# The 128 copies of a relative-position table are written from memory to memory, not from an 8-partition tile

## The chip, the core and the metric

One core of a Trainium2 chip runs the whole program as one launch. Its five engines (TensorE for matrix products, VectorE, ScalarE, GpSimd, and SyncE, which issues DMAs) each work through an instruction list of their own in order and wait for each other by semaphores. Data moves between memory and the on-chip SBUF by 16 DMA engines that all issuers share. The metric is the device time of one execution in microseconds (us).

## The reference

The program is one forward pass of two stacked transformer-like blocks on 256 tokens of width 1024, in float32. The stage that matters here is the first block's mixer, which projects the normalised input and feeds four branches:

```
proj = h @ w_in
(m_z, m_xbc, m_dt, b_qkv, c_qkv, c_f, d_q, d_kv, gate_logits) = split(proj)
y_a = mamba2_branch(m_z, m_xbc, m_dt, ...)          # a state-space scan with decays
y_b = moba_attention(bq, bk, bv, rel_bias[:, :8])   # one causal block of 256
y_c = forgetting_attention(cq, ck, cv, c_f + forget_bias)
y_d = sliding_window_attention(dq, dk, dv, sinks, rel_bias[:, 8:])
out = sum(sigmoid(gate_i) * (y_i @ w_branch_i)) @ w_out
```

`y_b` and `y_d` add to each attention score a bias that depends on the head and on the distance of query and key: `bias[h, q, k] = rel_bias[rel_bucket(q - k), h]`, for 8 heads each. For every query the 256 biases are a window of one table of 383 entries per head, shifted by one entry from query to query.

## The kernel before

All weights are streamed from memory in pieces of about 1 MB: SyncE loads a piece into one of four `raw` buffers (L138), ScalarE rounds it to a high part `whi` (L97), VectorE subtracts to get a low part `wlo` (L98), and TensorE makes three products of each pair (L143 to L145). `whi` and `wlo` have four buffers of half a piece each. A `raw` buffer is free for its next load once both halves are split. The order of the instructions on each engine is set by the framework's scheduler when the program is built; on the chip each engine keeps to it.

In the mixer, `mamba` first makes eight 128-column blocks of `m_xbc` (`gemm_b`). For each, VectorE writes the block into `xin` behind three zeros that GpSimd sets (L581, L582), applies a four-tap filter into `cv` (L568, L570), and ScalarE applies silu into `bcT` (four blocks) or `xsT` (four blocks) (L585). Behind these stands the call `then()`, which is `skew_bias`. Then come the products of `bcT` (L591, evicted as `cbm` at L594), the projection `m_z`, and, head by head, the decay factors `mt` from `rows` (L615 to L618). `rows` are the cumulated decays of four heads, which `rows4` has GpSimd load from a small memory array `acd`, once for heads 0 to 3 and once for 4 to 7 (L422). The query, key and value projections of the next branch (`qk`, L456) are interleaved with this.

`skew_bias` makes the bias. For each of the two groups of 8 heads, a product of the one-hot distance table and `rel_bias` gives [8 heads, 383] in PSUM (L382). VectorE copies it to the SBUF tile `rv` on 8 partitions (L384), and one DMA issued by GpSimd writes it 128 times per head into the memory array `skew[g]` (L385), 1024 rows of 1532 bytes. `rv` has one buffer, so the copy of the second group waits until the DMA of the first has read the tile. Later GpSimd loads each attention's bias from `skew` with a row step of 382 entries, which gives each query its shifted window (`bias4`, L432). GpSimd's DMAs are queued on q0; SyncE's on q1.

Of the kernel before, what the change touches and what calls it, by code (L numbers as in the profile page):

```python
# [9 lines left out]
F32 = mybir.dt.float32  # L10
# [6 lines left out]
P = 128  # L17
# [10 lines left out]
def bucket_onehot():  # L28
    """Per distance 255 - v the bucket of a relative position, for whole-block and windowed masks."""
    m = np.zeros((33, 2, NV), np.float32)  # L30
    for v in range(NV):
        d = 255 - v
        b = sum(1 for s in BUCKET_START if s <= max(d, 0)) - 1
        for g, lim in enumerate((256, 128)):
            if 0 <= d < lim:
                m[b, g, v] = 1.0
            else:
                m[32, g, v] = 1.0
    return m
# [8 lines left out]
def pack(inputs):  # L48
    """The program's inputs: the large arrays as they are, the small ones laid out in the columns of one array."""
    data = {n: np.ascontiguousarray(inputs[n]) for n in _INS}  # L50
    cols = []
    for name, n in COLS:
        c = np.zeros((P, n), np.float32)
        if name == "heads":
            c[0:8, 0] = inputs["dt_bias"][0]
            c[32:40, 0] = inputs["forget_bias"][0]
            c[0:8, 1] = inputs["a_log"][0]
        elif name == "rel_bias":
            c[0:32] = inputs["rel_bias"]
            c[32] = NEG  # L60
        elif n == 8 and inputs[name].size == 8:
            c[:] = np.asarray(inputs[name]).reshape(1, 8)
        else:
            c[:] = np.asarray(inputs[name]).reshape(n, P).T
        cols.append(c)
    data["params"] = np.ascontiguousarray(np.concatenate(cols, axis=1))
    w = np.zeros((P, 8, 40), np.float32)
    w[:, :, 0:8] = np.asarray(inputs["w_in"])[0, :, 1536:1544].reshape(8, P, 8).transpose(1, 0, 2)
    w[:, :, 32:40] = np.asarray(inputs["w_in"])[0, :, 4616:4624].reshape(8, P, 8).transpose(1, 0, 2)
    data["w_heads"] = w  # L70
    data["onehot"] = bucket_onehot()
    return data


class Build:
# [28 lines left out]
    def weights(self, dmas, nk, ncols):  # L104
        """Loads [128, nk, ncols] of weights by dmas(raw) and splits them; gives per K tile the pair (hi, lo)."""
        nc = self.nc
        raw = self.wraw.tile([P, 2048], F32, tag="raw", name=self.nm("raw"))
        r3 = raw[:, :nk * ncols].rearrange("p (k c) -> p k c", c=ncols)
        dmas(r3)
        out = []  # L110
        step = max(1, min(nk, 1024 // ncols))
        for k0 in range(0, nk, step):
            n = min(step, nk - k0)
            hi = self.wspl.tile([P, 1024], F32R, tag="whi", name=self.nm("whi"))
            lo = self.wspl.tile([P, 1024], F32R, tag="wlo", name=self.nm("wlo"))
            h3, l3 = (u[:, :n * ncols].rearrange("p (k c) -> p k c", c=ncols) for u in (hi, lo))
            with self.tc.high_priority(offset=400):
                self.split(h3, l3, r3[:, k0:k0 + n], self.split_engine())
            out += [(h3[:, k], l3[:, k]) for k in range(n)]
        return out  # L120

    def split_engine(self):
        """GpSimd takes a share of the weights' low parts where the vector engine has much else to do."""
        self.turn += 1
        if self.burst:
            self.burst -= 1
            return self.nc.gpsimd
        return self.nc.gpsimd if self.share and self.turn % self.share == 0 else self.nc.vector
# [18 lines left out]
    def gemm_a(self, hk, w, chunks, apart=0):  # L147
        """[tok, cols] = h @ w for the column chunks; chunks share the K order, so that early K tiles come first.
        Of the last `apart` K tiles the first token tile takes all before the second does."""
# [24 lines left out]
    def gemm_b(self, hk, w, c0, nblk):  # L174
        """[128 columns, 256 tok] blocks of (h @ w)^T."""
        wk = self.wunit(w, 0, 8, c0, nblk * P)
        return [self.block_b(hk, wk, slice(b * P, (b + 1) * P)) for b in range(nblk)]
# [10 lines left out]
    def norm_input(self, x, n, t, wcol, hi, lo, ss):  # L188
        """x[:, t, n-th half] -> sums of squares and the weighted, split transpose."""
# [17 lines left out]
    def held(self):  # L207
        """The first products of a phase take turns with the last transposes of its input."""
        ins = self.hold.pop(0) if self.hold else None
        return self.tc.issue_after(ins) if ins else nullcontext()  # L210
# [10 lines left out]
    def rstd(self, ss, scale=1.0 / D):  # L221
        """[128, 2] of rsqrt(mean of squares + eps) from the partial sums ss [128, 2, 2]."""
        nc = self.nc
        r = self.small.tile([P, 2], F32, tag="rstd", name=self.nm("rstd"))
        nc.vector.tensor_tensor(r, ss[:, :, 0], ss[:, :, 1], op=ALU.add)
        self.rsqrt(r, r, scale)
        return r
# [9 lines left out]
    def row(self, r):  # L237
        """Returns a function that gives [128, 256]: r of each token along the free axis, on every partition."""
# [19 lines left out]
    def to_T(self, src, hi, lo, t, nblk=4, scale=None, c0=0):  # L258
        """src [128 tok, nblk * 128] -> split transposes hi/lo[:, c0 + j, tokens of tile t]."""
# [15 lines left out]
    def constants(self):  # L275
# [9 lines left out]
        # causal factors for transposed scores: [s0 x l0 | s0 x l1 | s1 x l1]  # L285
# [19 lines left out]
    def swiglu(self, hk, r, wg, g0, wu, u0, wd, x, finish, apart=0):  # L305
        """x += (silu(h wg) * (h wu)) wd, with the norm's factor r applied to the products."""
# [39 lines left out]
    def project(self, hk, w, x, finish):  # L346
        """x += h @ w; the transposes of the first half's sum take place between the second half's products."""
# [12 lines left out]
    def mixer(self, hk, r, rr, x, finish):  # L360
        nc, a, tc = self.nc, self.a, self.tc
        w_in = a["w_in"][0]
        with tc.tile_pool(name="yT", bufs=3) as ytp, tc.tile_pool(name="att", bufs=1) as at, \
# [9 lines left out]
            skew = dr.tile([2, 8, P, NV], F32, name="skew")  # L373

            def skew_bias():
                # relative-position bias, [q, 255 + q - k] laid out along the diagonals
                oh = at.tile([33, 2, NV], F32, tag="pt", name="oh", bufs=1)
                nc.gpsimd.dma_start(oh, a["onehot"])
                rb = self.col["rel_bias"][0:33]
                for g in range(2):  # L380
                    ps = self.tp()
                    nc.tensor.matmul(ps[:8, :NV], rb[:, g * 8:(g + 1) * 8], oh[:, g], start=True, stop=True)  # L382
                    rv = at.tile([8, NV], F32, tag="y", name=self.nm("rv"), bufs=1)
                    nc.vector.tensor_copy(rv, ps[:8, :NV])  # L384
                    nc.gpsimd.dma_start(skew[g], rv.unsqueeze(1).to_broadcast([8, P, NV]))  # L385
# [3 lines left out]
            # m_dt and c_f side by side: [0:8] and [32:40] of one block of columns  # L389
# [85 lines left out]
            # sliding-window queries: block j holds heads j and j + 4  # L475
# [29 lines left out]
            def gate_evict(ps, c0, n, skip=0):  # L505
                """columns c0.. of the gate logits from ps[:, skip:]"""
# [46 lines left out]
    def softplus(self, out, v, e, w, d):  # L553
        """out = max(v, 0) + log1p(exp(-|v|)); the logarithm is corrected for the rounding of 1 + exp."""
# [10 lines left out]
    def conv4(self, out, xin, wcol, bcol):  # L565
        """Causal 4-tap filter along the free axis; xin has three zeros in front."""
# [70 lines left out]
    def attention(self, at, qT, kT, v, bias, own0, sinks, split_heads, yT):  # L637
        """Causal softmax attention of 8 heads of 64; bias(gi) holds bias and mask of a group of four heads."""
# [75 lines left out]
    def hgrn(self, hk, r, rr, x, finish):  # L714
        """Gated linear recurrence as decayed causal attention: pairs (t, s) are split by the level at which
        the halves that hold them part, so that both decay factors to the boundary are at most one."""
# [74 lines left out]
    def hgrn_scores(self, hp, q, k, f, masks, LV):  # L791
        """Transposed decayed scores of four heads.  At level L a token's q carries the decay from the start of
        its block of L tokens, its k the decay to the block's end; pairs in neighbouring blocks meet there."""
        nc = self.nc
        st = hp.tile([P, 4, 2, P], F32, tag="st", name=self.nm("st"), bufs=2)
        # s = t, on every partition; the identity keeps one
# [16 lines left out]
        for L in LV[::-1]:  # L813
# [4 lines left out]
            if L == 1:  # L818
                # neighbours, on every partition
# [55 lines left out]
    def lru(self, hk, r, rr, x, finish):  # L875
        nc, a, tc = self.nc, self.a, self.tc
        w = a["lru_w_in_2"][0]
        with tc.tile_pool(name="lru", bufs=1) as lp:
            cw, cb = self.col["lru_conv_w_2"], self.col["lru_conv_b_2"]
            ba, bx = self.col["lru_ba_2"], self.col["lru_bx_2"]  # L880
            # 8 softplus(-lambda)
# [41 lines left out]
            def decay(g):  # L923
                # a = exp(-c r);  1 - a^2 = tanh(c r) (1 + a^2)
# [43 lines left out]
            # the functions of one table stay together  # L968
# [22 lines left out]
    def body(self):  # L991
        nc, a, tc = self.nc, self.a, self.tc
        with ExitStack() as es:
# [37 lines left out]
            # the first block's final norm is the second block's input  # L1031
# [18 lines left out]
            # with m the mean square of x and m2 that of x * wf: rf^2 = 1 / (m + eps), r^2 = rf^2 / (m2 rf^2 + eps)  # L1050
# [76 lines left out]
```

## Time and profile before

| | |
|---|---|
| time, median of 3 runs | 1235.18 us (1235.17 to 1236.95) |
| span of the profiled execution | 1232.9 us |
| TensorE busy in the span | 1156.8 us (94%) |
| VectorE, ScalarE, GpSimd busy | 753.0, 600.4, 123.8 us |
| moved by DMA | 202.76 MB, mean 164 GB/s |

The span runs from the first to the last instruction of one profiled execution. That execution's own time outside the profiler is not recorded; the median of the timed runs is 2.3 us above the span. TensorE is the busiest engine by far, so what counts is where it stands idle or runs at a lower granted clock. Of the 40 equal slices of the span (30.8 us each), TensorE's busy digits are 8665 in the first four and 9 nearly everywhere else.

### The profile page before, as it was taken

How to read it: one execution, taken by the hardware profiler on the slowest of the kernel's cores; microseconds unless marked ns; L12 is line 12 of the kernel's file. 1: busy time of each engine (PE TensorE's matmuls, PEld its weight loads, DVE VectorE, ACT ScalarE, POOL GpSimd, SP SyncE). 2: the span in 40 equal slices, each digit the busy share in tenths (PEclk: the TensorE clock that was granted, in tenths of full speed). 3: DMA queues.
4: the chain of work that ended last, by engine and by line, in shares of the span. 5: the costliest groups of instructions: out<-in, count | busy, mean ns of one | idle time of the engine just before them, and what ended most of it. 6: DMA issues, size and time to landing. Idle time of an engine off the chain costs nothing.

```text
span 1232.9 us, 15797 instructions
## 1 busy us (share of the span) xinstructions
PE 1156.8 (94%) x6308; PEld 987.8 (80%) x6308; DVE 753.0 (61%) x968; ACT 600.4 (49%) x876; POOL 123.8 (10%) x118
## 2 busy tenths in 40 slices
PE   8665999999999999999999999999998769999997
PEld 7555989888888888888878878888888758888886
DVE  7373656556567555555899665555548795555553
ACT  6142656674445544445552455444445555544442
POOL 1000001000000000003820030000003432000000
PEclk9877999999999999999999999999999889999999
DMA  8676444535555555456443425555553544555550
GB/s 287 125 143 170 144 133 156 190 136 171 189 187 189 178 192 176 156 186 205 137 155 119 137 102 192 185 172 185 175 185 103 171 135 161 196 174 172 187 188 34
DMA packets 120729, 202.76 MB, mean 164 GB/s; under 512 B 4220, under 2 KB 44413, under 8 KB 120656
## 3 DMA queue, kind: packets, MB, share of 16 engines
q1 hardware_dynamic: 117264, 192.59, 47.1%
q0 software_dynamic: 2960, 8.53, 3.8%
q8 instruction: 49, 0.80, 0.3%
q10 hardware_dynamic: 432, 0.63, 0.2%
q14 instruction: 24, 0.20, 0.0%
HBM read 197.51 MB, written 4.23 MB: 164 GB/s over the span
## 4 chain that ended last, share of the span: by engine, by line
PE 82%; DVE 9%; DMA 6%; ACT 2%; issue 1%; SPq 0%; POOLq 0%; POOL 0%; DVEq 0%; ACTq 0%
PE acc L144 25%; PE acc L145 25%; PE acc L143 25%; DMA skew<-rv 3%; DMA raw<-in_w_in_dram 3%; DVE wlo L98 2%; PE tp L263 2%; PE tp L831 2%; DVE uc L570 1%; PE tp L661 1%; DVE hs L941 1%; ACT whi L97 1%; PE tp L690 1%; PE tp L197 1%; DVE sq L930 1%
## 5 line engine op out<-in xcount | busy, mean ns | idle before, releaser
L98 DVE TENSOR_TENSOR wlo<-raw,whi 128x1024 fp32r<-128x1024 f32 (+3 forms) x350 | 423.9, 1216 | 315.1 <-ACT whi L97 310.9
L97 ACT CAST whi<-raw 128x1024 fp32r<-128x1024 f32 (+3 forms) x372 | 382.1, 1032 | 409.9 <-PE acc L145 324.5
L145 PE MATMUL acc<-whi,hl 128*128 128x512 f32 (+2 forms) x832 | 318.2, 383 | 0.0
L144 PE MATMUL acc<-wlo,hh 128*128 128x512 f32 (+2 forms) x832 | 317.4, 382 | 0.6 <-DVE wlo L98 0.6
L143 PE MATMUL acc<-whi,hh 128*128 128x512 f32 (+2 forms) x832 | 313.0, 381 | 0.0
L144 PEld LDWEIGHTS acc<-wlo,hh 128*128 128x128 f32 x832 | 156.8, 188 | 33.2 <-DVE wlo L98 1.6
L143 PEld LDWEIGHTS acc<-whi,hh 128*128 128x128 f32 x832 | 156.9, 189 | 30.7 <-issue 0.3
L145 PEld LDWEIGHTS acc<-whi,hl 128*128 128x128 f32 x832 | 156.9, 189 | 30.2
L143 PE MATMUL acc<-hh,whi 128*128 128x256 f32 (+1 forms) x496 | 142.1, 289 | 27.7 <-ACT xsT L585 20.6
L145 PE MATMUL acc<-hh,wlo 128*128 128x256 f32 (+1 forms) x496 | 142.4, 289 | 3.5 <-DVE wlo L98 3.4
L144 PE MATMUL acc<-hl,whi 128*128 128x256 f32 (+1 forms) x496 | 142.6, 288 | 0.6 <-DVE hl L98 0.6
L143 PEld LDWEIGHTS acc<-hh,whi 128*128 128x128 f32 (+1 forms) x496 | 94.9, 192 | 30.0 <-ACT xsT L585 21.0
L144 PE MATMUL acc<-wlo,ah 128*128 128x512 f32 x264 | 102.5, 391 | 0.0
L145 PE MATMUL acc<-whi,al 128*128 128x512 f32 x264 | 102.0, 390 | 0.0
L143 PE MATMUL acc<-whi,ah 128*128 128x512 f32 x264 | 101.6, 390 | 0.0
L145 PEld LDWEIGHTS acc<-hh,wlo 128*128 128x128 f32 (+1 forms) x496 | 95.1, 192 | 5.2 <-DVE wlo L98 4.7
L98 POOL TENSOR_TENSOR wlo<-raw,whi 128x1024 fp32r<-128x1024 f32 x22 | 56.9, 2595 | 420.9 <-ACT whi L97 420.9
L144 PEld LDWEIGHTS acc<-hl,whi 128*128 128x128 f32 (+1 forms) x496 | 95.6, 193 | 2.6 <-DVE hl L98 1.1
L143 PEld LDWEIGHTS acc<-whi,ah 128*128 128x128 f32 x264 | 49.6, 188 | 10.2
L145 PEld LDWEIGHTS acc<-whi,al 128*128 128x128 f32 x264 | 49.6, 188 | 10.2
L144 PEld LDWEIGHTS acc<-wlo,ah 128*128 128x128 f32 x264 | 49.6, 188 | 10.0
L97 ACT CAST ah<-tp 128x512 fp32r<-128x512 f32 (+1 forms) x36 | 19.8, 550 | 34.6 <-PE tp L263 34.6
(307 smaller groups left out, 1286.1 us busy)
## 6 DMA issues: line engine op xcount, KB each, us to landing
raw<-in_ffn_w_in_dram SPq DMA_DIRECT2D x44, 1024.0 KB, 5.1
raw<-in_w_in_dram SPq DMA_DIRECT2D x33, 1024.0 KB, 5.0
raw<-in_ffn_w_out_dram SPq DMA_DIRECT2D x20, 1024.0 KB, 5.1
raw<-in_hgrn_w_in_dram SPq DMA_DIRECT2D x16, 1024.0 KB, 5.4
raw<-in_w_ffn_gate_dram SPq DMA_DIRECT2D x11, 1024.0 KB, 5.0
raw<-in_w_ffn_up_dram SPq DMA_DIRECT2D x11, 1024.0 KB, 5.0
raw<-in_w_ffn_down_dram SPq DMA_DIRECT2D x10, 1024.0 KB, 4.9
raw<-in_w_branch_dram SPq DMA_DIRECT2D x8, 1024.0 KB, 5.0
```

Source lines behind the costliest of these rows:

```text
L97: self.nc.scalar.copy(hi, src)
L98: (eng or self.nc.vector).tensor_tensor(lo, src, hi.bitcast(F32), op=ALU.subtract)
L143: mm(ps, sh, mh, start=start, stop=False)
L144: mm(ps, sh, ml, start=False, stop=False)
L145: mm(ps, sl, mh, start=False, stop=stop)
L197: last = nc.tensor.transpose(ps[:, j * P:(j + 1) * P], xc[:, j * P:(j + 1) * P], self.ident)
L263: nc.tensor.transpose(ps[:, j * P:(j + 1) * P], src[:, j * P:(j + 1) * P], self.ident)
L570: nc.vector.scalar_tensor_tensor(out, xin[:, k:k + S], wcol[k], out, op0=ALU.mult, op1=ALU.add)
L661: nc.tensor.matmul(ps[par][:, jj * W:(jj + 1) * W], qT[pr, 2 * gi + jj, qt * P:(qt + 1) * P], kT(2 * gi + jj)[pr, :W], start=True, stop=True)
L690: nc.tensor.transpose(ps[:, i * P:(i + 1) * P], sp[:, i, b * P:(b + 1) * P], self.ident)
L831: nc.tensor.matmul(ps[:, c:c + 64], k[:, h, ts], q[:, h, ts].rearrange("p (n u l) -> p n u l", u=2, l=L)[:, :, 1], start=True, stop=True)
L930: nc.vector.tensor_tensor(sq, av[g], av[g], op=ALU.mult)
```

## The change

The two tables are first collected in one tile `rv` of [8, 2, 383], which one DMA writes to a new small memory array `relv`. Two further DMAs then write the 128 copies of each group into `skew[g]`, with `relv` as their source instead of the SBUF tile. The destination, its layout and the loads from it are the same.

```diff
             skew = dr.tile([2, 8, P, NV], F32, name="skew")
+            relv = dr.tile([8, 2, NV], F32, name="relv")
...
                 rb = self.col["rel_bias"][0:33]
+                rv = at.tile([8, 2, NV], F32, tag="y", name="rv", bufs=1)
                 for g in range(2):
                     ps = self.tp()
                     nc.tensor.matmul(ps[:8, :NV], rb[:, g * 8:(g + 1) * 8], oh[:, g], start=True, stop=True)
-                    rv = at.tile([8, NV], F32, tag="y", name=self.nm("rv"), bufs=1)
-                    nc.vector.tensor_copy(rv, ps[:8, :NV])
-                    nc.gpsimd.dma_start(skew[g], rv.unsqueeze(1).to_broadcast([8, P, NV]))
+                    nc.vector.tensor_copy(rv[:, g], ps[:8, :NV])
+                nc.gpsimd.dma_start(relv, rv)
+
+                for g in range(2):
+                    nc.gpsimd.dma_start(skew[g], relv[:, g].unsqueeze(1).to_broadcast([8, P, NV]))
```

The other lines of the diff drop comments. Lines of the changed kernel stand four below those of before from here on (L581 is L585, L432 is L436). The scheduler orders the engines' instructions anew, of which three places follow. The numbers in the tile names below are counters of the build; a tile of the changed kernel has the number of its counterpart or one more.

GpSimd, from the first write of `skew` to the second load of `rows`, with the semaphores that each instruction waits for (`DMASW` is that of a DMA of GpSimd's own), before:

```order
L385 DMA skew<-rv_567 1024x1x383 [waits DVE_49]
L422 DMA rows_676<-acd 128x1024 [waits DMASW1_49]
L581 MEMSET xin_467 128x3 [waits DVE_49,Pool_49]
L581 MEMSET xin_476 128x3 [waits DVE_49,Pool_49]
L432 DMA bias_1109<-skew 128x4x256 [waits DMASW2_49]
L385 DMA skew<-rv_572 1024x1x383 [waits DVE_49]
L581 MEMSET xin_545 128x3 [waits DVE_49,Pool_49]
L581 MEMSET xin_554 128x3 [waits DVE_49,Pool_49]
L422 DMA rows_710<-acd 128x1024 [waits DMASW3_49,DVE_49]
```

and of the changed kernel:

```order
L426 DMA rows_677<-acd 128x1024 [waits DMASW1_49]
L386 DMA relv<-rv 8x766 [waits DVE_49]
L585 MEMSET xin_468 128x3 [waits DVE_49,Pool_49]
L585 MEMSET xin_477 128x3 [waits DVE_49,Pool_49]
L389 DMA skew<-relv 1024x1x383 [waits DMASW3_49]
L389 DMA skew<-relv 1024x1x383
L585 MEMSET xin_546 128x3 [waits DVE_49,Pool_49]
L436 DMA bias_1110<-skew 128x4x256 [waits DMASW4_49]
L585 MEMSET xin_555 128x3 [waits DVE_49,Pool_49]
L426 DMA rows_711<-acd 128x1024 [waits DMASW2_49,DVE_49]
```

The first `rows` load now stands ahead of the writes of `skew`; both of these stand together, behind a wait for `relv`; and one `xin` memset, `xin_555`, now stands behind the first bias load, which waits for the first write of `skew`.

VectorE around the copy of the second table, before:

```order
L98 TENSOR_TENSOR wlo_640<-raw_637,whi_639 128x1024
L582 TENSOR_TENSOR xin_476<-acc_442,rrow_223 128x256
L568 TENSOR_SCALAR cv_470<-xin_467,pcol 128x256
L98 TENSOR_TENSOR wlo_644<-raw_637,whi_643 128x1024
L568 TENSOR_SCALAR cv_479<-xin_476,pcol 128x256
L570 SCALAR_TENSOR_TENSOR cv_470<-xin_467,pcol,cv_470 128x256
L384 COPY rv_572<-tp_570 8x383
L570 SCALAR_TENSOR_TENSOR cv_479<-xin_476,pcol,cv_479 128x256
```

The changed kernel has both copies of `rv` earlier, one behind the other but for one split. The place at which it uses `xin_555` for the first time (`cv_558`) stands between the two halves of the piece `raw_785`, the first of the `qk` weights:

```order
L586 TENSOR_TENSOR xin_546<-acc_496,rrow_224 128x256
L574 SCALAR_TENSOR_TENSOR cv_480<-xin_477,pcol,cv_480 128x256
L572 TENSOR_SCALAR cv_549<-xin_546,pcol 128x256
L586 TENSOR_TENSOR xin_555<-acc_521,rrow_224 128x256
L98 TENSOR_TENSOR wlo_788<-raw_785,whi_787 128x1024
L574 SCALAR_TENSOR_TENSOR cv_549<-xin_546,pcol,cv_549 128x256
L572 TENSOR_SCALAR cv_558<-xin_555,pcol 128x256
L98 TENSOR_TENSOR wlo_792<-raw_785,whi_791 128x1024
L574 SCALAR_TENSOR_TENSOR cv_549<-xin_546,pcol,cv_549 128x256
```

So the filter that needs the memset is ahead of the second half's split `wlo_792` on VectorE.

ScalarE around the last silu of `bcT` (`bcT` of `cv_401` before, of `cv_402` now), before:

```order
L97 CAST whi_639<-raw_637 128x1024
L585 ACTIVATE bcT<-cv_392 128x256
L585 ACTIVATE bcT<-cv_401 128x256
L97 CAST whi_643<-raw_637 128x1024
L97 CAST whi_786<-raw_784 128x1024
```

and of the changed kernel:

```order
L97 CAST whi_640<-raw_638 128x1024
L589 ACTIVATE bcT<-cv_393 128x256
L97 CAST whi_644<-raw_638 128x1024
L621 ACT_TABLE_LOAD
L621 ACTIVATE mt_679<-mt_679 128x384
L621 ACTIVATE mt_687<-mt_687 128x384
L589 ACT_TABLE_LOAD
L589 ACTIVATE bcT<-cv_402 128x256
```

The exponentials of `mt` for the first two heads, with a table load ahead and another behind, now stand in front of the last `bcT`. On TensorE the products of `bcT` stand at the same place among the `m_z` products in both.

## Rows read from the trace of the kernel before

**Rows 1.** The first line of the page of the kernel before, and its part 4: the chain that ended last, by engine and by line, as shares of the span.

```profile
span 1232.9 us, 15797 instructions
...
PE 82%; DVE 9%; DMA 6%; ACT 2%; issue 1%; SPq 0%; POOLq 0%; POOL 0%; DVEq 0%; ACTq 0%
PE acc L144 25%; PE acc L145 25%; PE acc L143 25%; DMA skew<-rv 3%; DMA raw<-in_w_in_dram 3%; DVE wlo L98 2%; PE tp L263 2%; PE tp L831 2%; DVE uc L570 1%; PE tp L661 1%; DVE hs L941 1%; ACT whi L97 1%; PE tp L690 1%; PE tp L197 1%; DVE sq L930 1%
```

**Rows 2.** The waits of TensorE from 25 to 140 us: who waited for whom, us in total, times, the longest.

```profile
PE acc L143 <- ACT xsT L585: 20.6, 1, 20.6
PE tp L620 <- DVE mt L618: 13.3, 1, 13.3
```

**Rows 3.** Stretches of the trace (from:to in us): length, busy time and instruction count of each engine, then the granted TensorE clock as a share of full speed, the busy share of the 16 DMA engines, and GB/s.

```profile
52.00:72.80 20.80, 0.28 (x2) 0.00 (x0) 3.87 (x10) 0.78 (x3) 2.21 (x4) 0.55 0.55 104
72.80:78.10 5.30, 5.00 (x22) 4.73 (x23) 5.30 (x12) 5.07 (x7) 0.00 (x0) 0.50 0.77 114
78.10:102.60 24.50, 23.89 (x202) 23.53 (x201) 15.22 (x27) 10.35 (x14) 0.55 (x1) 1.00 0.73 131
102.60:115.90 13.30, 0.05 (x2) 0.03 (x1) 4.25 (x9) 3.19 (x5) 0.00 (x0) 0.61 0.66 198
115.90:122.50 6.60, 6.60 (x23) 5.83 (x24) 5.36 (x11) 2.72 (x4) 0.00 (x0) 0.50 0.63 200
```

**Rows 4.** The timeline of VectorE (DVE): start in us, duration in us, line, operation, out<-in, count, and in brackets the idle time before and what ended it.

```profile
33.72 0.54 DVE L384 COPY rv<-tp 8x383 f32<-8x383 f32 x1
...
42.65 0.48 DVE L570 SCALAR_TENSOR_TENSOR cv<-xin,pcol,cv 128x256 f32<-128x256 f32 x1
68.93 0.55 DVE L384 COPY rv<-tp 8x383 f32<-8x383 f32 x1 [25.80 <-DMA skew<-rv]
...
75.67 1.20 DVE L98 TENSOR_TENSOR wlo<-raw,whi 128x1024 fp32r<-128x1024 f32 x1
...
111.46 1.23 DVE L98 TENSOR_TENSOR wlo<-raw,whi 128x1024 fp32r<-128x1024 f32 x1 [16.34 <-ACT whi L97]
```

**Rows 5.** The timeline of GpSimd (POOL), columns as in rows 4; for a DMA the duration is that of the issue.

```profile
30.17 0.59 POOL L408 DMA_DIRECT2D acd<-dt  x1 [1.81 <-DVE dt L406]
...
34.56 1.11 POOL L385 DMA_DIRECT2D skew<-rv  x1 [3.21 <-DVE rv L384]
35.66 0.59 POOL L422 DMA_DIRECT2D rows<-acd  x1
...
69.20 0.78 POOL L432 DMA_DIRECT2D bias<-skew  x1 [30.72 <-DMA skew<-rv]
...
72.50 0.24 POOL L581 MEMSET xin<- 128x3 f32 x1 [0.29 <-DVE cv L570]
```

**Rows 6.** DMA issues of six short stretches (30 to 31, 34 to 36, 42 to 44, 69 to 71, 76 to 78 and 91 to 94 us): out<-in, queue, count, KB of each, us from issue to landing.

```profile
acd<-dt POOLq DMA_DIRECT2D x1, 40.0 KB, 4.6
...
skew<-rv POOLq DMA_DIRECT2D x1, 1532.0 KB, 34.4
raw<-in_w_in_dram SPq DMA_DIRECT2D x1, 1024.0 KB, 35.9
...
raw<-in_w_in_dram SPq DMA_DIRECT2D x1, 1024.0 KB, 33.3
...
skew<-rv POOLq DMA_DIRECT2D x1, 1532.0 KB, 37.5
...
raw<-in_w_in_dram SPq DMA_DIRECT2D x1, 1024.0 KB, 33.4
...
rows<-acd POOLq DMA_DIRECT2D x1, 512.0 KB, 17.2
```

**Rows 7.** DMA queues (q0 takes GpSimd's DMAs, q1 those of SyncE): packets, MB, and the time of their packets as a share of 16 engines over the stretch. First 48 to 66 us (18 us), in which `skew<-rv` runs; then q0 from 163.4 to 172 us (8.6 us), the load `bias<-acd`, whose source is one 4 KB stretch of memory read for all 128 partitions (128 packets, the others being a few bytes); then q1 from 1224 to 1233 us (9 us), half of the store of the output (256 packets of 2 KB).

```profile
q0 software_dynamic: 192, 0.88, 47.1%
q1 hardware_dynamic: 192, 0.20, 3.1%
...
q0 software_dynamic: 144, 0.52, 15.8%
...
q1 hardware_dynamic: 288, 0.52, 15.7%
```

**Rows 8.** The timeline of TensorE (PE), columns as in rows 4.

```profile
42.64 1.47 PE L591 MATMUL tp<-bcT 128*128 128x256 f32 x8
...
51.88 0.40 PE L145 MATMUL acc<-whi,hl 128*128 128x512 f32 x1
72.86 0.55 PE L143 MATMUL acc<-hh,whi 128*128 128x256 f32 x1 [20.59 <-ACT xsT L585]
...
78.83 0.28 PE L143 MATMUL acc<-hh,whi 128*128 128x256 f32 x1
78.94 0.28 PE L144 MATMUL acc<-hl,whi 128*128 128x256 f32 x1
```

**Rows 9.** The timeline of ScalarE (ACT), columns as in rows 4.

```profile
39.27 0.72 ACT L585 ACTIVATE bcT<-cv 128x256 f32<-128x256 f32 x2
39.90 1.03 ACT L97 CAST whi<-raw 128x1024 fp32r<-128x1024 f32 x1
...
73.79 1.28 ACT L617 ACT_TABLE_LOAD   x1
75.08 0.94 ACT L617 ACTIVATE mt<-mt 128x384 f32<-128x384 f32 x2
```

## The prediction

> **What bounds the kernel now.** The page's chain of work that ended last comes first: TensorE has 82% of it, and among the shares by line stand 3% for the DMA `skew<-rv` and 3% for a load of weights [rows 1], two times about 37 us in which TensorE was not the limit. The list of TensorE's waits shows where: within 25 to 140 us it waits twice for long, 20.6 us and 13.3 us [rows 2]. The stretches show what each costs in all. [...] Work at half clock counts half, so the first hole costs 20.6 + 2.6 = 23.2 us, the second 13.3 + 3.3 = 16.6 us.
>
> Both end with a write of `skew`. In the first, VectorE's copy of the second table waits 25.80 us for the first `skew<-rv` to release the one `rv` buffer, and all weight splits queue behind it on VectorE [rows 4]. GpSimd waits 30.72 us for the same DMA before it can issue the bias load [rows 5]. In the second, no engine waits for `skew` by name. A piece of weights takes 33.4 us from issue to landing, `rows` takes 17.2 us, and VectorE sits 16.34 us before the split of that piece [rows 4, 6]. These are loads that share DMA engines with the second write, which itself takes 37.5 us [rows 6].
>
> Why is the write so slow? From 48 to 66 us it has 47.1% of 16 engines, so about 8 of them, for 192 packets and 0.88 MB: 4.6 KB a packet (three copies of 1532 bytes), 0.471 x 16 x 18 / 192 = 0.706 us each, or 6.5 GB/s per busy engine. The weights get as many packets (192) in that time, of 0.046 us each: they pass one by one between packets of `skew` [rows 7]. Other DMAs are far from that. The load `bias<-acd`, which reads one stretch of memory again and again, has 0.52 MB in 0.158 x 16 x 8.6 = 21.7 us of engine time, 24 GB/s per engine; the store of the output has 0.52 MB in 22.6 us, 23 GB/s [rows 7]. Neither reading a memory stretch repeatedly nor writing memory from many partitions is slow here, so I take the source on 8 partitions as the cause; but the rows of 1532 bytes, which no other DMA has, are not excluded.
>
> [...]
>
> **The change, step by step.** *`relv`.* VectorE's first copy ends at 34.3 us, a split of 1.2 us and the second copy of 0.54 us follow, so `rv` is full at about 35.9 [rows 4]. The 24 KB write to `relv` is taken at the 4.6 us of `acd<-dt` (40 KB) [rows 6]. The first write of `skew` is then issued at 40.6 us, 6 us later than now, the second behind it.
>
> *The write of `skew`.* Of its present 34.4 us, 43 packets per engine at 0.706 + 0.046 are 32.3; start and landing are the other 2.1. The trace has no memory-to-memory DMA. From below, a packet costs what 24 GB/s give, 0.19 us; if reading and writing add up, 0.39 (0.19 + 0.20); from above, if the write of 1532-byte rows is the limit, 0.706 as now. The nearest rows are the read and the store, so I take 0.3, between their overlap and their sum. The first write lands at 40.6 + 2.1 + 43 x 0.346 = 57.6 us (ends: 52.8, 61.4, and 75 at the present rate). The outermost count of the source is still 8, so I leave it on 8 engines; this makes no difference to the first write, only to whether the second runs beside or behind it.
>
> *What waits for it now.* No VectorE copy does. But GpSimd issues the first bias load when `skew[0]` has landed, 0.78 us, and only behind that sets `xin_555`, 0.24 us at most [rows 5]. On VectorE `cv_558` needs that memset, and the split `wlo_792` is queued behind it: landing + 1.0 + 0.4 + 1.2 + 0.1, so `wlo_792` is ready 2.7 us after the landing, at 60.3.
>
> *TensorE until there.* Now it ends `m_z` at 52.3 [rows 8]. The last `bcT` on ScalarE stands behind two table loads of 1.28 and the exponentials of 0.94 us; these follow a rounding that ended at 40.9, so `bcT` is done at 40.9 + 3.5 + 0.1 = 44.5, and its products, at 42.64 now, come 1.9 us later [rows 8, 9]. `m_z` ends at 54.2. Then 24 products with the first half of `raw_785`, one every 0.12 us, and four transposes take 3.2 us: at 57.4 it needs `wlo_792`. It reached this point at 78.9 before [rows 8]. Waiting to 60.4 it gains 18.5, less about 1.3 us for a lower clock after so short a wait (0 to 2.6): **17.2 us**. At 0.19 us a packet nothing waits: 21.5. At 0.39: 78.9 - 64.2 - 2.6 = 12.1. At 0.706: 78.9 - 77.8 - 2.6 = -1.5.
>
> *The second hole.* TensorE restarts with four pieces loaded or landing with the end of the write, one in each `raw` buffer. The last two are those that are issued from 34 to 36 and from 42 to 44 us now and then held for 35.9 and 33.3 us [rows 6]; of these the first now lands before the writes begin. Half a piece is 24 products or 2.8 us, so 3.5 pieces cover 20 us. The next load, issued at about 60, needs even beside a second write only 32 packets of 2 KB per engine, under 15 us. The second load of `rows` is issued some 20 us after the restart and meets no `skew` any more. So the second hole goes: **16.6 us**.
>
> Sum: 33.8 us; VectorE's other work and the copies into `rv` (the same two) cost nothing while TensorE has products in hand. Against the span: 1232.9 - 33.8 = 1199.1; the median stands 2.3 us above the span, which gives 1201.4. From the fifth slice of the page on TensorE is at 9 tenths nearly throughout, so what is gained here is not waited away later.
>
> **Rivals.** *The rate does not change, the two writes run beside each other on 16 engines* (the 1532-byte rows are the limit): the first landing is at 75, the first hole costs 1.5 more than now, the second is gone: -15 us, 1220. For it: no other DMA has such rows. Against: the store's 23 GB/s. *The rate does not change and both writes queue on the same 8 engines*, so that the change does not do what it says: the second lands at 42.7 + 86 x 0.752 = 107.4, where it ends now (70.0 + 37.5); the second hole stays, and the first is no shorter: 1233 to 1236, no change.
>
> *Slower*: the path from memory to memory is slower per packet than the tile was. If both writes share 8 engines, the landing of the second passes the present 107.5 from 0.71 us a packet on; at 1.0 us it is 42.7 + 86 x 1.046 = 132.7, 25 us later, 1260. If they run beside each other, it takes 1.06 us to lose anything. For it only that no row shows such a transfer.
>
> [...]
>
> **How the numbers follow.** The likeliest case, a faster packet and no second hole, gets 0.74; its own range is 1196 (0.19 us a packet: 38.1 us saved) to 1207 (0.39: 28.7). The first rival gets 0.09, a rate between 0.4 and 0.7 us or another hole of about 10 us, for 1222 to 1231, 0.05, the second rival 0.04, slower 0.08. The range of 1195 to 1221 holds the first two, 0.83. A change of 0.2%, 2.5 us, is about what a measurement of this kernel can tell from none: faster 0.88, same 0.04, slower 0.08. The forecast is 1201 us.
>
> **What would show it.** Right: `skew<-relv` has packets of 0.2 to 0.4 us; its first issue is near 40.6 us and lands by 62; VectorE's longest wait before 70 us is at the filter behind `xin_555`, released by GpSimd; TensorE's holes before 130 us sum to under 8 us. Wrong: the packets stay at 0.7 us or more; the holes come back further on because loads of weights still take over 25 us from issue to landing; or `rows` or `relv` land so late that VectorE stops before 50 us.

## The result and the profile after

The changed kernel takes 1206.14 us (median of 4 runs, 1204.1 to 1207.34), the kernel before 1235.18 (4 runs beside them): a ratio of 0.9766, 95% interval 0.9752 to 0.9781. It is 2.3% faster. The forecast was 1201 us, in a range of 1195 to 1221. The profiled execution has a span of 1205.6 us against 1232.9, a gain of 27.3 us where the sum said 33.8; the medians lie 29.0 us apart, and the profiled execution (1207.34 us) is the slowest of its four.

The first line of the page and the chain that ended last, which answer to [rows 1]:

```profile
span 1205.6 us, 15797 instructions
...
PE 84%; DVE 10%; issue 3%; ACT 1%; DMA 1%; POOL 0%; SPq 0%; POOLq 0%; DVEq 0%; ACTq 0%
PE acc L144 25%; PE acc L145 25%; PE acc L143 25%; DVE wlo L98 3%; PE tp L263 2%; PE tp L835 2%; DVE uc L574 1%; PE tp L665 1%; DVE hs L945 1%; PE tp L694 1%; PE tp L197 1%; DVE sq L934 1%; ACT whi L97 1%; DMA rows<-acd 1%; PE tp L702 0%
```

By name, `skew` and the held load of weights, 3% each before, are no longer among these lines, and DMA has 1% of the chain instead of 6%. But the first write of `skew` still holds the chain, under another name. "issue" has 3% instead of 1%, and between 25 and 75 us the longest piece of the chain (start, duration) is one of these:

```profile
50.68 12.83 issue
```

In this time GpSimd waits for that write, as its timeline below shows. TensorE's waits from 25 to 140 us, which answer to [rows 2], and stretches of the trace with the columns of [rows 3]:

```profile
PE acc L145 <- DVE wlo L98: 8.5, 1, 8.5
PE tp L595 <- ACT bcT L589: 1.9, 1, 1.9
```

```profile
45.30:57.60 12.30, 12.30 (x67) 10.41 (x67) 8.47 (x18) 4.65 (x6) 1.02 (x2) 1.00 0.86 188
57.60:66.10 8.50, 0.04 (x2) 0.02 (x1) 1.61 (x3) 0.00 (x0) 0.93 (x2) 0.72 0.99 217
66.10:71.60 5.50, 5.50 (x26) 5.50 (x27) 5.50 (x9) 1.93 (x4) 0.00 (x0) 0.50 1.01 339
71.60:100.00 28.40, 28.40 (x215) 27.02 (x215) 20.69 (x39) 15.46 (x20) 0.55 (x1) 1.00 0.60 196
100.00:140.00 40.00, 40.00 (x309) 37.16 (x308) 28.35 (x49) 21.07 (x49) 2.29 (x3) 1.00 0.46 146
```

The two holes, the stretches of 20.6 and 13.3 us in which TensorE waited, have become one of 8.5 us, from 57.6 to 66.1, with 5.5 us at half clock (0.50) behind it. From 71.6 to 140 us TensorE is busy throughout; the second hole is gone. Where the one hole comes from, the timelines of GpSimd and then VectorE show (columns as in [rows 4, 5]):

```profile
36.28 0.52 POOL L386 DMA_DIRECT2D relv<-rv  x1
...
43.44 0.10 POOL L585 MEMSET xin<- 128x3 f32 x1 [5.66 <-DVE cv L574]
44.00 2.22 POOL L389 DMA_DIRECT2D skew<-relv  x2 [0.46 <-issue]
...
63.52 0.82 POOL L436 DMA_DIRECT2D bias<-skew  x1 [12.85 <-DMA skew<-relv]
64.33 0.12 POOL L585 MEMSET xin<- 128x3 f32 x1
```

```profile
35.28 0.54 DVE L385 COPY rv<-tp 8x383 f32<-8x383 f32 x1
...
41.92 0.35 DVE L619 TENSOR_SCALAR mt<-rows,tcol 128x256 f32<-128x256 f32 x1 [3.64 <-DMA rows<-acd]
...
64.48 0.41 DVE L572 TENSOR_SCALAR cv<-xin,pcol 128x256 f32<-128x256 f32 x1 [10.72 <-POOL xin L585]
64.81 1.22 DVE L98 TENSOR_TENSOR wlo<-raw,whi 128x1024 fp32r<-128x1024 f32 x1
```

VectorE's copy into `rv` waits for no DMA now. The wait that remains goes through GpSimd: the bias load waits 12.85 us for the first write of `skew`, the memset of `xin` stands behind the bias load, the filter behind the memset, and the split for TensorE behind the filter. The DMA issues from 35 to 37 and 46 to 47 us answer to [rows 6], queue q0 from 48 to 60 us, where both writes run, to [rows 7]:

```profile
rows<-acd POOLq DMA_DIRECT2D x1, 512.0 KB, 6.2
relv<-rv POOLq DMA_DIRECT2D x1, 23.9 KB, 5.8
...
raw<-in_w_in_dram SPq DMA_DIRECT2D x1, 1024.0 KB, 21.5
...
q0 software_dynamic: 478, 2.18, 86.9%
```

0.869 x 16 x 12 / 478 = 0.349 us a packet, half of the 0.706 of before, and on nearly twice the engines (86.9% of 16 against 47.1%): 2.18 MB in 12 us are 182 GB/s, against 49 before (0.88 MB in 18 us [rows 7]).

### The profile page after: what moved, and what is told of

It is laid out like the page before. It is cut to its first block, busy times and chain, and to the rows that moved or that the text cites. A ratio compares the mean times of both kernels' runs of the same rounds, so it can differ in the third digit from the quotient of the medians.

```text
span 1205.6 us, 15797 instructions
## 1 busy us (share of the span) xinstructions
PE 1155.0 (96%) x6308; PEld 986.4 (82%) x6308; DVE 753.3 (62%) x968; ACT 600.8 (50%) x876; POOL 124.2 (10%) x119
## 4 chain that ended last, share of the span: by engine, by line
PE 84%; DVE 10%; issue 3%; ACT 1%; DMA 1%; POOL 0%; SPq 0%; POOLq 0%; DVEq 0%; ACTq 0%
PE acc L144 25%; PE acc L145 25%; PE acc L143 25%; DVE wlo L98 3%; PE tp L263 2%; PE tp L835 2%; DVE uc L574 1%; PE tp L665 1%; DVE hs L945 1%; PE tp L694 1%; PE tp L197 1%; DVE sq L934 1%; ACT whi L97 1%; DMA rows<-acd 1%; PE tp L702 0%
```

## The experiments

Times are medians of 4 runs (8 for the one that edits the kernel before by its memsets alone); ratios are to the kernel before on the same chip, whose medians there were 1232.6 to 1234.8 us.

**Only the wait taken away.** The kernel before with one tile for both tables, both writes still from its 8 partitions.

```
+                rv = at.tile([8, 2, NV], F32, tag="y", name="rv", bufs=1)
                 for g in range(2):
...
-                    rv = at.tile([8, NV], F32, tag="y", name=self.nm("rv"), bufs=1)
-                    nc.vector.tensor_copy(rv, ps[:8, :NV])
-                    nc.gpsimd.dma_start(skew[g], rv.unsqueeze(1).to_broadcast([8, P, NV]))
+                    nc.vector.tensor_copy(rv[:, g], ps[:8, :NV])
+                for g in range(2):
+                    nc.gpsimd.dma_start(skew[g], rv[:, g].unsqueeze(1).to_broadcast([8, P, NV]))
```

> The kernel before with the one new tile for both tables, so that VectorE's second copy waits for no write; both writes of `skew` still leave from the 8 partitions of that tile, and there is no `relv`. Theory A (the rate of the write is what counts, and the 8 partitions set it): packets of 4.6 KB take 0.7 us if the writes queue on the same engines, about 1.3 us if they run side by side and share the source. The first write then lands between 70 and 92 us, GpSimd's bias load and the memsets behind it wait for that, and the first hole of TensorE stays (about 20 us) or grows; weights still take over 25 us from issue to landing. The time is 1225 to 1245 us. Theory B (what counts is the wait of VectorE for the single `rv` buffer): the 25.80 us wait is gone and with it most of both holes, 1202 to 1210 us.

Measured: 1247.14 us, ratio 1.0113 (1.0089 to 1.0137), so 1.1% slower. The issues from 35 to 38.5 us, then q0 from 48 to 92 us, then the longest waits of VectorE and of TensorE from 25 to 140 us:

```profile
skew<-rv POOLq DMA_DIRECT2D x2, 1532.0 KB, 68.0
raw<-in_w_in_dram SPq DMA_DIRECT2D x1, 1024.0 KB, 68.4
rows<-acd POOLq DMA_DIRECT2D x1, 512.0 KB, 67.3
...
q0 software_dynamic: 484, 2.22, 95.9%
...
DVE mt L616 <- DMA rows<-acd: 56.8, 2, 56.6
...
PE acc L143 <- DVE xin L583: 51.8, 1, 51.8
```

The writes run side by side on all 16 engines (95.9%), and each packet takes 0.959 x 16 x 44 / 484 = 1.395 us, twice as long as on 8 engines. The rate is 2.22 MB / 44 us = 50 GB/s, as before: the source sets it, and engines add nothing. Theory B falls: with VectorE's wait for `rv` gone, TensorE waits 51.8 us in one piece, where its two waits before were 33.9 us together. The prediction's first rival counted on two writes beside each other passing twice as much; from this tile they do not. Theory A had the mechanism right but the size too small: its landing of up to 92 us became 102, and the time is 2 us above its range of 1225 to 1245, which lay on both sides of no change. VectorE was held not through GpSimd's bias load but by `rows`, which is issued behind the first write on the same queue (67.3 us from issue to landing, 34.9 in the kernel before).

**The 8 rows spread over the partitions.** The kernel before with a widened stationary operand, so that head h stands on partition 16h; everything else, the single buffer too, stays.

```
+                rb16 = at.tile([33, 16, 16], F32, name="rb16")
+                nc.vector.tensor_copy(rb16, rb.unsqueeze(2).to_broadcast([33, 16, 16]))
...
-                    nc.gpsimd.dma_start(skew[g], rv.unsqueeze(1).to_broadcast([8, P, NV]))
+                    r8 = rv.rearrange("(h j) v -> h j v", j=16)[:, 0:1]
+                    nc.gpsimd.dma_start(skew[g], r8.to_broadcast([8, P, NV]))
```

> The kernel before with each table's 8 rows on partitions 0, 16, ..., 112 instead of 0 to 7; still one `rv` buffer, still a write from that tile, still rows of 1532 bytes, the same order and the same queue. Theory A (8 neighbouring partitions of the tile set the rate): packets fall from 0.706 us to 0.2 to 0.35 us, the first write lands at 48 to 52 us instead of 68.8, VectorE's wait of 25.80 us shrinks to under 9 us, both holes are nearly gone, and the time is 1194 to 1206 us, without any write from memory to memory. Theory C (the rows of 1532 bytes, or that a tile is the source at all, set the rate): packets stay at 0.7 us and the time at 1233 to 1237 us.

Measured: 1205.53 us, ratio 0.9777 (0.9759 to 0.9794). Queue q0 from 46 to 52 us and VectorE's wait before the second copy:

```profile
q0 software_dynamic: 130, 0.60, 45.4%
...
DVE rv L387 <- DMA skew<-rv: 12.8, 1, 12.8
```

0.454 x 16 x 6 / 130 = 0.335 us a packet, 100 GB/s: twice the rate from the same 8 rows of 1532 bytes, from a tile, with one buffer. Theory C falls. The change could have had all of its gain without any copy in memory. Nor is it the new order of the instructions that gains: GpSimd's order in this run, from the first write to the second load of `rows`, is that of the kernel before. The first write landed at 56.1 us (48 to 52 expected), and the wait of 12.8 us is above the 9 expected.

**The same, 4 partitions apart**, with `[33, 16, 4]` and `j=4` in the edit above.

> The kernel before with each table's 8 rows on partitions 0, 4, ..., 28; still one `rv` buffer and the write from that tile, as in the run with partitions 0, 16, ..., 112, where packets took 0.336 to 0.42 us. [...] Theory E (what counts is how far apart the rows lie): 4 apart is worse than 16 apart, packets take 0.4 to 0.65 us and the time is 1208 to 1230 us.

Measured: 1198.73 us, ratio 0.9706 (0.9691 to 0.9721). Queue q0 from 41 to 45 us:

```profile
q0 software_dynamic: 194, 0.83, 54.4%
```

Some packets here are smaller ones, of `rows`, so the rate per busy engine is the cleaner measure: 0.83 MB / (0.544 x 16 x 4 us) = 23.8 GB/s, 0.19 us for 4.6 KB. Nearer together is faster, so distance is not what counts (theory E falls). For a packet as short as that of a write from memory alone (0.206 us in the run below that holds the second write back), the author's estimate was 0.17 to 0.22 us, a landing at 46 to 49 us, a wait of VectorE under 5 us and a time of 1194 to 1201 us: packet and time are inside, the landing at 49.3 us and VectorE's wait of 5.1 us just outside. With the rows on 0 to 7, 16 apart and 4 apart, the write ran at 49, 100 and about 190 GB/s (the last an estimate, 8 engines at 23.8); per engine the last is the pace of the load of `bias`, 24 GB/s [rows 7]. What sets the three rates apart is not shown: all three writes have a tile as the source and rows of 1532 bytes, and the rates do not follow the distance.

**The memsets on VectorE.** The changed kernel with one word changed.

```
-                nc.gpsimd.memset(xin[:, 0:3], 0.0)
+                nc.vector.memset(xin[:, 0:3], 0.0)
```

> The changed kernel with the memsets of `xin` on VectorE, so that no memset stands behind GpSimd's bias load. Theory A (what is left of the first hole is this queue): VectorE's 10.72 us wait at the filter goes, TensorE's 8.5 us wait with it, and the granted clock does not fall to 0.50 after it: 1206 - 8.5 - 2.8 = 1195, 1193 to 1198 us. Also the writes of `skew` are issued about 1.5 us earlier, since no memset stands ahead of them. Rival: TensorE runs into the piece of weights that takes 21.5 us beside the writes (landing at 67.8 us in the changed kernel) and waits there instead: 1202 to 1207 us.

Measured: 1196.15 us, ratio 0.971 (0.9683 to 0.9736). TensorE's only waits from 25 to 140 us, and GpSimd's timeline:

```profile
PE tp L624 <- DVE mt L622: 2.3, 2, 1.2
```

```profile
35.34 0.52 POOL L386 DMA_DIRECT2D relv<-rv  x1 [1.31 <-DVE tcol L419]
40.73 2.22 POOL L389 DMA_DIRECT2D skew<-relv  x2 [4.88 <-DMA relv<-rv]
61.04 0.82 POOL L436 DMA_DIRECT2D bias<-skew  x1 [18.08 <-DMA skew<-relv]
```

Theory A holds. The writes leave at 40.73 us instead of 44.00, 3.3 us earlier where 1.5 were expected. The first still takes 20 us (GpSimd's wait ends at 61.04), but no engine that TensorE needs waits for it. The span, 1193.1, is 39.8 us below 1232.9, as much as the prediction priced the two holes at (23.2 + 16.6). That the figures meet is luck: the profiled execution is the fastest of its four, the medians (1232.55 and 1196.15) lie 36.4 us apart, and the prediction's own sum for a write that holds nothing up is 38.1.

**The same edit on the kernel before.**

> The kernel before with the memsets of `xin` on VectorE, and nothing else. Theory: in the kernel before this queue was hidden, since VectorE stood still for the single `rv` buffer in the same time; VectorE's wait of 25.8 us at the second copy stays, and the time is 1230 to 1237 us. The 9 us that the same edit gave to the changed kernel exist only once the other wait is gone. Rival (the edit is worth its 9 us anywhere): 1222 to 1227 us.

Measured: 1236.99 us, ratio 1.002 (1.0008 to 1.0033): no gain, but a loss of 0.1 to 0.3%. VectorE's wait for `rv` is where it was:

```profile
DVE rv L384 <- DMA skew<-rv: 26.4, 1, 26.4
```

So the queue behind the bias load became a limit only when the wait for `rv` had gone.

**The second write held back.** The changed kernel with `skew[1]`, which only the last attention reads, written behind the first attention's bias loads (`loads` collects the bias loads as they are issued).

```
+                skew_write(0)
+
+            def skew_write(g):
+                nc.gpsimd.dma_start(skew[g], relv[:, g].unsqueeze(1).to_broadcast([8, P, NV]))
...
+            with tc.issue_after(loads[-1]):
+                skew_write(1)
             qT2, kT2, v2 = load_qkv(3080)
```

> The changed kernel with the second write of `skew` held until GpSimd has issued the two bias loads of the first attention, so that the first write runs without it. Theory A (the two writes slow each other): packets of the first write fall from 0.3 to 0.38 us to 0.18 to 0.22, it lands at 54 to 57 us instead of 63.2, TensorE's wait of 8.5 us falls to under 2, and the time to 1195 to 1200 us. Rival (they run on engines of their own and do not touch each other): packets and landing stay, 1204 to 1208 us; if the late write then holds weights in its turn, 1206 to 1215.

Measured: 1200.81 us, ratio 0.9735 (0.9718 to 0.9752). Queue q0 from 50 to 56 us, the load of weights issued at 46.3 us, TensorE's longest wait:

```profile
q0 software_dynamic: 188, 0.85, 40.4%
...
raw<-in_w_in_dram SPq DMA_DIRECT2D x1, 1024.0 KB, 12.5
...
PE acc L145 <- DVE wlo L98: 1.7, 1, 1.7
```

A write alone on its engines has packets of 0.404 x 16 x 6 / 188 = 0.206 us, 22 GB/s per engine; with the second beside it they take 0.349. Theory A holds: the two slow each other. The first write landed at 57.2 us and the time is 1200.81, both just above theory A's ranges. The late write is issued at 109.7 us and lands 16.4 us later beside weights; TensorE waits for nothing from 100 to 140 us.

**The copies outermost.** The changed kernel with source and destination turned, so that the outermost dimension counts 128 instead of 8.

```
-                    nc.gpsimd.dma_start(skew[g], relv[:, g].unsqueeze(1).to_broadcast([8, P, NV]))
+                    nc.gpsimd.dma_start(skew[g].rearrange("h p v -> p h v"),
+                                        bass.AP(relv.tensor, relv.offset + g * NV, [[0, P], [2 * NV, 8], [1, NV]]))
```

> The changed kernel with the 128 copies as the outermost dimension of source and destination, the 8 heads inside. Theory A2 (the count of the outermost dimension decides on how many engines a write goes): each write now takes all 16 engines, so the second queues behind the first on the same engines; packets are of 1532 bytes. If the two writes together cannot pass about 190 GB/s (16 x 4596 bytes in 0.38 us, as in the changed kernel), the first still gets all of it: issue 44 + 1.1 + 2 + 8.3, landing at 54 to 57 us instead of 63.2, the second near 64 to 67 as now. TensorE's wait of 8.5 us falls to under 2.5 and the time to 1196 to 1202 us. Rival: each write stays on 8 engines, or the smaller packets eat the gain: landing at 62 us or later, 1205 to 1212 us.

Measured: 1197.17 us, ratio 0.9701 (0.9685 to 0.9717). Queue q0 from 46 to 50 us, in which the first write runs:

```profile
q0 software_dynamic: 164, 0.73, 96.8%
```

One write now fills 16 engines (96.8%; 47.1% before [rows 7]), and the second queues behind it: they land at 53.6 and 60.6 us, earlier than expected. The rate is 0.73 / 4 = 182 GB/s, what the two had together when side by side. The packets stayed at some 4.5 KB (0.73 MB / 164), not the 1.5 KB expected.

**All 128 partitions.** The kernel before with each row on 16 partitions, written 8 times from each, both tables in one tile, no `relv`, the memsets on VectorE.

```
+                rv = at.tile([P, 2, NV], F32, tag="y", name="rv", bufs=1)
...
+                    nc.gpsimd.dma_start(skew[g].rearrange("h (j c) v -> (h j) c v", j=16),
+                                        rv[:, g].unsqueeze(1).to_broadcast([P, 8, NV]))
```

> The kernel before with each head's row on 16 partitions, so that all 128 are the source and each row is written 8 times; both tables in one tile, no `relv`, the memsets of `xin` on VectorE. Theory D: nothing holds a packet but its engine, 0.19 to 0.22 us, on 16 engines for each write; issued at about 34 us, both have landed by 50 us. No weights are held, TensorE waits nowhere before 140 us for over 2 us: 1188 to 1195 us, below the 1196 of the changed kernel with the memsets on VectorE, since acd, rows and the tables wait for nothing from memory in between. Rival (writes into memory are themselves limited to about 190 GB/s, as two writes from memory side by side were): packets of 0.35 to 0.4 us, both landed at 53 to 56 us, still hidden, 1193 to 1198 us.

Measured: 1197.3 us, ratio 0.9706 (0.9683 to 0.973). Queue q0 from 36 to 38 us, when the first write begins, and from 38 to 42 us, in which it goes on, and TensorE's only wait:

```profile
q0 software_dynamic: 147, 0.68, 96.7%
q0 software_dynamic: 162, 0.74, 88.2%
...
PE tp L606 <- ACT xsT L590: 1.4, 1, 1.4
```

From 38 to 42 us, 0.882 x 16 x 4 / 162 = 0.348 us a packet and 185 GB/s: the rival holds. In the first 2 us it was 0.21 us and 340 GB/s, theory D's packet, so what limits the write sets in only behind its start. From then on sixteen engines writing into this array pass no more from a tile than from memory (185 and 182 GB/s), so it is not the reading of `relv` that limits two writes. The writes landed at 44.8 and 54.8 us. TensorE waits 1.4 us in all from 25 to 140 us, so little was left to win.

**Memsets on VectorE and the second write held**, both edits on the changed kernel.

> The changed kernel with both edits, the memsets of `xin` on VectorE and the second write of `skew` held until the first attention's bias loads are issued. Theory: the two holes of the kernel before were worth 23.2 + 16.6 = 39.8 us, and the run with the memsets alone already has them all (its span is 1193.1, 39.8 below 1232.9), so that nothing is left here: span 1191 to 1196 us, median 1194 to 1198, though the first write lands at 52 to 55 us instead of 60.8 and the weights beside it in under 14 us instead of 18 to 22. Rival (the transfers beside the two writes still cost the tail of something): 1188 to 1192 us.

Measured: 1193.39 us (1191.3 to 1195.89), ratio 0.9661 (0.9644 to 0.9678), the best of all; the span of its profiled execution is 1194.2. TensorE is busy for 114.86 of the 115 us from 25 to 140:

```profile
25.00:140.00 115.00, 114.86 (x819) 104.45 (x818) 86.30 (x162) 65.98 (x122) 8.91 (x12) 1.00 0.60 193
```

The median lies between the ranges of the theory and the rival. With the memsets alone the ratio was 0.971 (0.9683 to 0.9736), and TensorE was busy for 112.66 of these 115 us. The two intervals do not overlap, but they lie only 0.0005 apart, the runs of the kernel before beside them differ (medians 1234.28 and 1232.55 us), and the two profiled spans stand the other way round (1194.2 and 1193.1). Whether the held write adds something there is not settled.

## Why the prediction was right, and where it missed

**The cause.** The source on 8 neighbouring partitions set the rate; taking it away shortened both holes. The runs with rows spread over the tile show this without any memory copy, and the run that only took the wait away shows that the wait was not it. Rows of 1532 bytes, which the prediction could not exclude, are excluded as the cause of the 0.706 us a packet.

**Up to the issue: wrong by 3.4 us.** `rv` is full at 35.8 us (35.9 computed). `relv` took 5.8 us, not the 4.6 of `acd<-dt`; it is issued 0.6 us behind `rows` (6.2 us). The larger part is an order that the prediction did not look at, though the list of GpSimd's instructions shows it: ahead of the two writes stands a memset of `xin`, which runs at 43.44 us, since it waits for a filter that VectorE could not make while it waited 3.64 us for `rows`. That stop of VectorE before 50 us was named as a sign of something wrong, but not priced. Without the memsets on GpSimd the writes left at 40.73 us, against 40.6 computed.

**The packet: the sum was nearly right for a reason that was not.** I took 0.3 us as a mean of overlap (0.19) and sum (0.39) of reading and writing. Alone, a memory-to-memory packet took 0.206 us (188 packets, 0.85 MB, with the second write held), near the estimate for an overlap and far from that for the sum. Side by side they took 0.349, because two writes hold each other up, which I had excluded with the sentence that the width makes no difference to the first write. The landing came 19.2 us after the issue instead of 17.0, at 63.2 us instead of 57.6.

**From there to TensorE: right.** `wlo` was ready at 66.0, 2.8 us after the landing (2.7 computed), through the queue that was named. TensorE stops at 57.6 (57.4 computed):

```profile
45.27 0.92 PE L595 MATMUL tp<-bcT 128*128 128x256 f32 x4 [1.86 <-ACT bcT L589]
...
57.35 0.28 PE L143 MATMUL acc<-hh,whi 128*128 128x256 f32 x1
66.09 0.58 PE L145 MATMUL acc<-hh,wlo 128*128 128x256 f32 x1 [8.46 <-DVE wlo L98]
```

Its wait for `bcT` is 1.9 us, as computed, but that is luck. On ScalarE the last `bcT` ended at 45.2 us and not at 44.5, since the exponentials waited 0.46 us for VectorE and `bcT` itself, counted at 0.1, took 0.42:

```profile
42.50 0.98 ACT L621 ACTIVATE mt<-mt 128x384 f32<-128x384 f32 x2 [0.46 <-DVE mt L620]
43.50 1.28 ACT L589 ACT_TABLE_LOAD   x1
44.80 0.42 ACT L589 ACTIVATE bcT<-cv 128x256 f32<-128x256 f32 x1
```

Against this, only four of the eight products had to wait for it; the other four ran from 42.59 to 43.40 us. The two errors cancel.

**The clock: mis-sized.** After the wait the granted clock was 0.50 for 5.5 us. Counted as half, as the prediction counts the 5.30 and 6.60 us at 0.50 of [rows 3] in its 2.6 and 3.3 us, this cost 2.8 us, not 1.3; by the matmuls of 128x256, one every 0.213 us there and every 0.118 at 1.00, about 2.5. The wait had become 8.5 us instead of 3. After waits under 2 us, with the second write held, the mean clock of the stretch from 25 to 140 us was 1.00 (longest wait 1.7 us).

**The second hole: right**, 16.6 us gone, here and in every run with a faster source. The sum with the measured terms: 78.9 - 66.1 - 2.8 + 16.6 = 26.6 us, against 27.3 in the spans. Of the 33.8 us computed, 5.7 went to the later restart and 1.5 to the clock; TensorE's holes before 130 us add up to 10.4 us, where the prediction said under 8. Three slips in the prediction change nothing: the two pieces of the chain called about 37 us are 34.35 and 33.40; 38.1 us saved would be 1197 and not 1196; and the timed execution that was profiled stands 1.7 us above its span (1207.34 and 1205.6), where the sum added 2.3.

**The rivals.** *Rate unchanged* (both forms): the packets are 0.35 us and not 0.706. What the first of them assumed of the engines is what happened: the two writes ran beside each other, on 86.9% of 16. *Slower*: alone, the memory path took 0.206 us a packet, under a third of the tile's 0.706.

**The width.** The prediction left the write on 8 engines because 8 stand outermost. The runs show it so: with 8 outermost a write had 47.1% of 16 before, 45.4% with the rows 16 apart and 40.4% from memory without the second beside it; with 128 outermost, 96.8% from memory and 88.2 to 96.7% from a tile. For the gain the width counted little: the two writes together passed 182 GB/s either way. What it did hide is the order: on 16 engines the first write lands 12 us after its issue, and 19 us after it when it runs on part of them beside the second.

## What to carry over

Before adding a hop through memory, look at which partitions feed a DMA with few rows: the same 8 rows went at 49, 100 and about 190 GB/s by their place alone. When a wait is removed, read in order what each waiting engine has queued in front of the next DMA issue; the memsets on GpSimd cost 7 us (by the ratios) to 10 us (by the medians) here, and nothing in the kernel before. A transfer that has time belongs behind the one that doesn't, since here two side by side took 19.2 and 21.7 us from issue to landing, and 13.2 and 16.4 us with the second held back.

## What was not expected of the hardware

Sixteen engines that write into this memory array moved 182 to 185 GB/s, as a mean of stretches of 4 to 12 us, in three forms: two writes on 8 engines each and one write on 16 engines, both from memory, and one on 16 engines from a tile. Per busy engine that is 12 to 13 GB/s (2.18 MB / (0.869 x 16 x 12 us) and so on), against 22 where 8 engines wrote from memory. The total is no higher than 8 engines at their pace from rows 4 partitions apart (8 x 23.8, about 190 GB/s), so in that run a limit of the engines and a limit of this total can't be told apart. The total is no fixed pace either: from 36 to 38 us the write from 128 partitions moved 340 GB/s. What sets it stays open; the runs exclude reading `relv` as its cause, and other row lengths or row starts were not tried. Eight neighbouring partitions gave 49 to 50 GB/s whether 8 or 16 engines drew on them.
